# The rotation of the queries: three of its five vector steps computed on GpSimd, the factor 2^-13 moved into the tables

## The chip, the cores and the metric

The kernel runs on one core of a Trainium2 chip. The metric is the device time of one execution in microseconds (us). A core has TensorE (PE in the profile) for matrix products, VectorE (DVE), ScalarE (ACT) and GpSimd (POOL) for work along rows, and a queue of transfers issued by SyncE (SP). The engines run side by side, each through its own list of instructions in order; an instruction whose input is not ready holds up everything behind it on its engine.

## The reference

The reference is a trunk of two layers over 2048 tokens of width 1024. Each layer normalises its input, multiplies it by one wide matrix `w_in`, and splits the result into a recurrent branch, an attention branch and a pooling branch. These are gated, joined, multiplied by `w_out` and added to the input. A last normalisation follows the second layer.

The change concerns the attention branch, cut here to what matters:

```python
q = (rms_norm(c_q, q_norm_g) @ w_uq).reshape(B, S, MLA_HEADS, QK_NOPE_DIM + QK_ROPE_DIM)
q_nope = q[..., :QK_NOPE_DIM]
q_rope = apply_rope(q[..., QK_NOPE_DIM:], cos, sin)
...
s = (einsum(q_nope, k_nope) + einsum(q_rope, k_rope)) * scale   # causal, softmax, times v
```

There are six heads with 64 plain and 32 rotated elements each. The rotation takes the two halves x1, x2 of the 32 and returns x1 cos - x2 sin and x1 sin + x2 cos, with tables of cos and sin over the positions.

## The kernel before, in words

Numbers of 32 bits are split into two halves of 16 bits, a high and a low part, and a product is the sum of three products of 16-bit halves. So nearly every result that PE leaves in PSUM is followed by two operations: ACT writes the high part, DVE subtracts it from the value and writes the low part.

Tokens are worked in four chunks of 512 (C), heads in three pairs (p). A layer runs in stages: the products with `w_in` (`zgroup`, line 397), with the branches' own work interleaved; then the keys, values and queries of the attention; then scores, softmax and values for each chunk of queries and pair of heads (`scores`, `finish`), with the output product interleaved. Before the scores of a chunk and pair, `row_max` (lines 799 to 821) computes a bound for each row's maximum: PE multiplies high parts, DVE takes maxima straight from PSUM (L804, L806), and the result goes through DRAM into row 96 of the tile `kq`.

`q_rope(x, tag)` (line 763 on) makes the rotated part of the queries for one pair of heads and two chunks. It is called six times per layer: once in `early`, which runs between the last products with `w_in`; once in the list `rest` behind them; and four times in `later_queries`, during the first attention units. Its steps:

1. SP loads the tables `ct` and `sn`, each 128x512 in 32 bits.
2. PE makes eighteen products into the PSUM tile `qrp` (L772).
3. DVE swaps the halves of each group of 32 rows, from PSUM into the SBUF tile `qsw` (L780).
4. DVE multiplies `qrp` by 2^-13 and by `ct` (L781, the first product), and `qsw` by 2^-13 and by `sn` (L782, the second product), and adds the two into `ct` (L783, the sum).
5. ACT writes the sum's high part into the tile `pr` (L785), DVE the low part (L786).
6. SP sends `pr` to its rows of `kq` in four transfers (L788), each with both parts.

The rotation of the keys, `krope`, runs once per layer and already multiplies on GpSimd (L631, L632). GpSimd's other work is small: gains times weights (L221), ones beside the values (L748), and the fill of row 96 in `head_tiles` (L711).

The order on each engine is not simply that of the program text. `spawn`, `tick` and `between` interleave generators while the program is written down, and the framework's planner then places the instructions of each engine by priority and by when its cost model thinks that their inputs are ready. Thus the trace shows other instructions between the steps of one rope. The tiles `ct`, `sn`, `qsw`, `pr` and many others share seven buffers (tag `t`).

Of the kernel before, what the change touches and what calls it, by code (L numbers as in the profile page):

```python
# [14 lines left out]
ALU = mybir.AluOpType  # L15
# [31 lines left out]
RUNITS = [((p, c), (p, c + 1)) for p in range(3) for c in range(0, NC, 2)]  # L47
# [8 lines left out]
def body(nc, tc, a, ctx):  # L56
# [11 lines left out]
    def T(name, dt=F32):  # L68
        return tp.tile([128, 512], dt, tag="t", bufs=7, name=name)

    def PS(tag, name):
        return psum.tile([128, 512], F32, tag=tag, bufs=BANKS[tag], name=name)
# [317 lines left out]
    def zgroup(st, m, c, few):  # L390
        w, sc = st["zw"][m]
        zbank[0] += 1
        ps = PS("mm" if few else ("mm", "mm", "po", "mm", "su")[zbank[0] % 5], "zps")
        n = 0
        for k in range(KD):
            for i, j in PASSES:
                nc.tensor.matmul(  # L397
                    ps[:], w[:, i, k, :], st["h"](j, k, c), start=n == 0, stop=n == 3 * KD - 1
                )
                n += 1  # L400
            if k % FINE == FINE - 1:
                between()
        return ps, sc

    def layer(st):
# [357 lines left out]
        def q_rope(x, tag):  # L763
            units = RUNITS[x]
            ps = PS(tag, "qrp")
            ct, sn, qs = T("ct"), T("sn"), T("qsw")
            nc.sync.dma_start(ct[:], a["rq"][x, 0])
            nc.sync.dma_start(sn[:], a["rq"][x, 1])
            for n in range(9):
                k, (i, j) = n // 3, PASSES[n % 3]  # L770
                for u, (p, c) in enumerate(units):
                    nc.tensor.matmul(  # L772
                        ps[64 * u : 64 * u + 64, :],
                        wq[p][:, i, k, 128:192],
                        hats["q"][:, j, k, CS[c]],
                        start=n == 0,
                        stop=n == 8,
                        tile_position=(0, 64 * u),
                    )
            nc.vector.stream_shuffle(qs[:], ps[:], mask=swap)  # L780
            nc.vector.scalar_tensor_tensor(ct[:], ps[:], 2.0 ** -13, ct[:], ALU.mult, ALU.mult)  # L781
            nc.vector.scalar_tensor_tensor(sn[:], qs[:], 2.0 ** -13, sn[:], ALU.mult, ALU.mult)  # L782
            nc.vector.tensor_tensor(ct[:], ct[:], sn[:], ALU.add)  # L783
            t = tp.tile([128, 2, 512], F16, tag="t", bufs=7, name="pr")
            nc.scalar.activation(t[:, 0, :], ct[:], AF.Copy)  # L785
            nc.vector.tensor_tensor(t[:, 1, :], ct[:], t[:, 0, :], ALU.subtract)  # L786
            for g, (p, c, h) in enumerate([(p, c, h) for p, c in units for h in range(2)]):
                nc.sync.dma_start(kq[p][64:96, h, 2:4, CS[c]], t[32 * g : 32 * g + 32, :, :])  # L788

# [52 lines left out]
        def early():  # L842

            for t in range(6):
                values_of(t, "ax")
                yield 1
                yield 1
            head_tiles(0, big, "A")
            for c in range(NC):
                keys(0, c, "ax")  # L850
                yield 1
            for c in range(2):
                while lat.get(("q", c)) != "done":
                    yield 1
                query(0, c, "ax")
                yield 1
            q_rope(0, "ax")
            yield 1
            for qc in range(2):
                yield from row_max(qc, 0, 3)  # L860
                maxed.add((qc, 0))
# [46 lines left out]
        for g, (m, c) in enumerate(groups):  # L908
# [13 lines left out]
            ps, sc = zgroup(st, m, c, g < g1)  # L922
# [31 lines left out]
        for p in (1, 2):  # L954
            for n in range(5):
                rest += [lambda p=p, n=n: keys(p, n, bank())] if n < NC else []
                rest += [lambda t=5 * p + n + 1: values_of(t, bank())]
            if p < QE:
                rest += [lambda p=p: query(p, 0, bank()), lambda p=p: query(p, 1, bank())]
                rest += [lambda p=p: q_rope(2 * p, bank()), lambda p=p: have.add((p, 0))]  # L960
# [308 lines left out]
def arrange(x, norm_g, w_in, conv_w, conv_b, w_rg, b_rg, w_ig, b_ig, lru_lambda,  # L1269
            q_norm_g, w_uq, kv_norm_g, w_ukv, w_pool, pool_scale, w_out, final_norm_g):  # L1270
    f = np.float32
    A = lambda v: np.ascontiguousarray(np.asarray(v))
    ins, par = {}, {}
    ins["x"] = A(np.asarray(x)[0])
    w_in = np.asarray(w_in)

    starts = [0, 128, 256, 384, 512, 640, 1152, 1280, 768, 896, 1024, 1824, 1952, 2080, 2208, 1440, 1568, 1696]
    wk_ = w_in.reshape(L, KD, 128, w_in.shape[2]).transpose(0, 2, 1, 3)
    ins["win"] = A(np.stack([wk_[:, :, :, s : s + 128] for s in starts], axis=1))
    ins["wkr"] = A(wk_[:, :, :, 1408:1440])  # L1280
    par["ng"] = A(np.asarray(norm_g).reshape(L, KD, 128).transpose(2, 0, 1))
    prm = np.zeros((128, L, 3, 8), f)
    per = lambda v: np.asarray(v).reshape(L, 3, 128).transpose(2, 0, 1)
    for t in range(4):
        prm[:, :, :, t] = per(np.asarray(conv_w)[:, t])
    for i, v in enumerate((conv_b, b_rg, b_ig, lru_lambda)):
        prm[:, :, :, 4 + i] = per(v)

    gb = prm[:, :, :, 5:7].reshape(2, 64, L, 3, 2)
    prm[:, :, :, 5:7] = gb.transpose(4, 1, 2, 3, 0).reshape(128, L, 3, 2)  # L1290
    par["prm"] = prm
    wg = np.zeros((L, 3, 128, 2, 128), f)
    for g, w in enumerate((np.asarray(w_rg), np.asarray(w_ig))):
        for h in range(6):
            c = slice(64 * g, 64 * g + 64)
            wg[:, h // 2, 0:64, h % 2, c] = wg[:, h // 2, 64:128, h % 2, c] = w[:, h]
    ins["wg"] = wg
    wp = np.zeros((L, 2, 128, 128), f)
    for g in range(4):
        r = 64 * (g % 2)  # L1300
        wp[:, g // 2, r : r + 64, r : r + 64] = np.asarray(w_pool)[:, g]
    ins["wp"] = wp
    par["pscl"] = A(np.asarray(pool_scale).reshape(L, 2, 128).transpose(2, 0, 1))
    par["kg"] = A(np.asarray(kv_norm_g).reshape(L, 2, 128).transpose(2, 0, 1))
    par["qg"] = A(np.asarray(q_norm_g).reshape(L, 3, 128).transpose(2, 0, 1))
    ins["fgb"] = A(np.broadcast_to(np.asarray(final_norm_g), (128, D)))
    uq = np.asarray(w_uq).reshape(L, 3, 128, 3, 2, 96).transpose(0, 3, 2, 1, 4, 5)
    ins["wuq"] = A(
        np.concatenate(
            [uq[..., :64].reshape(L, 3, 128, 3, 128), uq[..., 64:].reshape(L, 3, 128, 3, 64)], axis=-1  # L1310
        )
    )
    ukv = np.asarray(w_ukv).reshape(L, 2, 128, 6, 128).transpose(0, 2, 1, 3, 4)
    ins["wukv"] = A(
        np.concatenate(
            [ukv[..., :64].reshape(L, 128, 2, 384), ukv[..., 64:].reshape(L, 128, 2, 384)], axis=-1
        )
    )
    ins["wout"] = A(np.asarray(w_out).reshape(L, KD, 128, D))

    pos = np.arange(S, dtype=f)
    inv = f(10000.0) ** (-np.arange(0, 32, 2, dtype=f) / f(32))
    ang = (pos[:, None] * inv[None, :]).astype(f)
    cos, sin = np.cos(ang).astype(f).T, np.sin(ang).astype(f).T
    c32, s32 = np.concatenate([cos, cos]), np.concatenate([-sin, sin])
    two = lambda t, c: np.tile(t[:, C * c : C * c + C], (2, 1))
    ins["rq"] = A(np.stack([np.stack([np.concatenate([two(t, c) for _, c in u]) for t in (c32, s32)]) for u in RUNITS]))
    rows = lambda t: A(t.reshape(32, NC, C).transpose(1, 0, 2).reshape(128, C))
    ins["cosk"], ins["sink"] = rows(c32), rows(s32)
    p = np.arange(128)  # L1330
    tri = np.where(p[None, :] > p[:, None], f(-1e36), f(0)).astype(f)
    ins["masks"] = A(np.concatenate([np.eye(128, dtype=f), tri, tri.T], axis=1))
    rc = np.zeros((128, 2, 17), f)
    for g, w in enumerate((2, 4, 8, 16)):
        r = 64 * (g % 2)
        rc[r : r + 64, g // 2, 0:16] = w / np.minimum(np.arange(1, 17), w)
        rc[r : r + 64, g // 2, 16] = 1.0 / w
    par["rcnt"] = rc
    ins["par"] = A(np.concatenate([par[n].reshape(128, -1) for n in PAR], axis=1))
    return ins  # L1340
# [22 lines left out]
```

## Time and profile before

| What | Value |
|---|---|
| median of 3 runs | 1963.67 us (1960.27 to 1965.01) |
| profiled execution, own time | 1963.13 us |
| its span, first to last instruction | 1961.3 us |
| mean granted TensorE clock | 0.991 |
| PE busy | 1890.0 us, 96% |
| DVE busy | 1439.5 us, 73% |
| ACT busy | 1163.4 us, 59% |
| POOL busy | 45.6 us, 2%, 38 instructions |

A busy time is the sum of the stretches in which the engine computed. Matrix products overlap in the engine's pipeline, so PE's busy time says when PE had work, not that it was at its peak. A wait is written `A <- B`: the instruction A was released by B. The tile before the arrow `<-` inside a name is the one written, those behind it are read.

### The profile page before, as it was taken

How to read it: one execution, taken by the hardware profiler on the slowest of the kernel's cores; microseconds unless marked ns; L12 is line 12 of the kernel's file. 1: busy time of each engine (PE TensorE's matmuls, PEld its weight loads, DVE VectorE, ACT ScalarE, POOL GpSimd, SP SyncE). 2: the span in 40 equal slices, each digit the busy share in tenths (PEclk: the TensorE clock that was granted, in tenths of full speed). 3: DMA queues.
4: the chain of work that ended last, by engine and by line, in shares of the span. 5: the costliest groups of instructions: out<-in, count | busy, mean ns of one | idle time of the engine just before them, and what ended most of it. 6: DMA issues, size and time to landing. Idle time of an engine off the chain costs nothing. (4 is left out here: it accounts for less than half of the span.)

```text
span 1961.3 us, 32926 instructions
## 1 busy us (share of the span) xinstructions
PE 1890.0 (96%) x12352; PEld 981.0 (50%) x12352; DVE 1439.5 (73%) x3310; ACT 1163.4 (59%) x2095; POOL 45.6 (2%) x38
## 2 busy tenths in 40 slices
PE   8999999999889999999999999999998999999998
PEld 4444444444455555555454444444444555555553
DVE  6757788767898787774385567878687977987745
ACT  8877877644355455465386678775434644644641
POOL 0000000010000000000000000001010000000000
PEclk8999999999999999999999999999999999999999
DMA  6313242212453121122741223331234621421444
GB/s 204 119 49 113 78 139 100 62 33 63 102 167 128 44 92 43 46 76 68 250 152 63 81 93 99 116 106 46 49 76 103 200 77 44 151 87 55 162 152 145
DMA packets 125281, 197.75 MB, mean 101 GB/s; under 512 B 18752, under 2 KB 41536, under 8 KB 125120
## 3 DMA queue, kind: packets, MB, share of 16 engines
q1 hardware_dynamic: 125120, 195.64, 31.8%
q8 instruction: 97, 1.59, 0.3%
q14 instruction: 64, 0.52, 0.1%
HBM read 124.59 MB, written 55.26 MB: 92 GB/s over the span
## 5 line engine op out<-in xcount | busy, mean ns | idle before, releaser
L397 PEld LDWEIGHTS <-zw 128*128 128x128 f16 x3456 | 336.3, 99 | 395.8 <-issue 21.3
L1030 ACT ACTIVATE p<-sps,tiny,sig 128x512 f32<-128x512 f32 x480 | 321.5, 709 | 327.2 <-PE sps L1027 174.9
L397 PE MATMUL zps<-hA,zw 128*128 128x512 f16 x1728 | 396.3, 383 | 0.3 <-DVE hA L355 0.2
L397 PE MATMUL zps<-hB,zw 128*128 128x512 f16 x1728 | 382.6, 379 | 0.0
L1104 PE MATMUL ops<-wo,yb 128*128 128x512 f16 x1536 | 368.5, 379 | 6.4 <-DVE xr L1096 4.8
L1031 DVE TENSOR_TENSOR pl<-p 128x1024 f16<-128x1024 f32 x240 | 254.0, 1059 | 126.3 <-ACT p L1030 100.3
L1104 PEld LDWEIGHTS <-yb 128*128 128x128 f16 x1536 | 144.5, 97 | 171.2 <-issue 8.2
L804 DVE TENSOR_REDUCE mx<-pm 128x1 f32<-128x512 f32 x288 | 192.6, 683 | 21.9 <-PE pm L799 21.8
L1025 PE MATMUL sps<-kq 97*128 97x512 f16 x480 | 167.0, 348 | 3.0 <-ACT p L1030 2.8
L1026 PE MATMUL sps<-kq 96*128 96x512 f16 x480 | 166.6, 347 | 0.0
L1027 PE MATMUL sps<-kq 96*128 96x512 f16 x480 | 165.7, 345 | 0.0
L799 PE MATMUL pm<-kq 96*128 96x512 f16 (+3 forms) x496 | 151.0, 345 | 5.0 <-DVE mx L804 2.5
L1044 PE MATMUL av<-zw,p 128*128 128x129 f16 (+1 forms) x1632 | 140.2, 214 | 5.2 <-ACT ar L994 5.2
L1044 PEld LDWEIGHTS <-p 128*128 128x128 bf16 x1632 | 108.5, 98 | 30.3 <-PE sps L1029 1.0
L806 DVE CUSTOM_DVE_ANT_0 pm<-pm,mkq 128x128 f32<-128x128 f32 (+1 forms) x208 | 101.1, 495 | 12.7 <-PE pm L799 11.8
L1044 PE MATMUL av<-zw,pl 128*128 128x65 f16 x1632 | 92.9, 194 | 1.7 <-DVE pl L1031 1.7
L1044 PEld LDWEIGHTS <-pl 128*128 128x128 f16 x1632 | 75.1, 98 | 12.2 <-DVE pl L1031 8.3
L1026 PEld LDWEIGHTS <-kq 96*128 96x128 f16 x480 | 47.2, 98 | 43.4 <-issue 5.1
L1027 PEld LDWEIGHTS <-kq 96*128 96x128 f16 x480 | 47.1, 98 | 43.6 <-issue 1.9
L1025 PEld LDWEIGHTS <-kq 97*128 97x128 f16 x480 | 46.6, 97 | 44.0 <-issue 4.2
L485 ACT ACTIVATE lsa<-pg,gp 64x512 f32<-64x512 f32 x96 | 65.2, 679 | 1.6
L1049 PE MATMUL av<-zw,p 128*128 128x64 f16 x336 | 64.8, 193 | 0.0
(300 smaller groups left out, 2613.2 us busy)
## 6 DMA issues: line engine op xcount, KB each, us to landing
xk<-x SPq DMA_DIRECT2D x80, 256.0 KB
raw<-win SPq DMA_DIRECT2D x72, 256.0 KB
raw<-wout SPq DMA_DIRECT2D x64, 256.0 KB
yr<-y SPq DMA_DIRECT2D x64, 256.0 KB
xr<-x SPq DMA_DIRECT2D x56, 256.0 KB
x<-xr SPq DMA_DIRECT2D x56, 256.0 KB
sg<-sg SPq DMA_DIRECT2D x48, 256.0 KB
kq<-pq SPq DMA_DIRECT2D x96, 128.0 KB
```

Source lines behind the costliest of these rows:

```text
L397: nc.tensor.matmul(ps[:], w[:, i, k, :], st["h"](j, k, c), start=n == 0, stop=n == 3 * KD - 1)
L485: nc.scalar.activation(t_[o], pg[h, :], AF.Tanh, scale=0.5, bias=gp[h, l, j, b : b + 1])
L799: nc.tensor.matmul(pm[:, 0:n], t[0:96, h, 2, q0 : q0 + 128], t[0:96, h, 0, s * C : s * C + n], start=True, stop=True)
L804: nc.vector.tensor_reduce(m, pm[:], AX.X, ALU.max)
L806: nc.vector.tensor_tensor_reduce(out=pm[:, 0:n], in0=pm[:, 0:n], in1=mkq[:, C - n : C], op0=ALU.add, op1=ALU.max, scale=1.0, scalar=-3.0e3 ...
L1025: nc.tensor.matmul(ps[:, o:C], t[0:97, h, 0, ks], t[0:97, h, 2, qs], start=True, stop=False)
L1026: nc.tensor.matmul(ps[:, o:C], t[0:96, h, 0, ks], t[0:96, h, 3, qs], start=False, stop=False)
L1027: nc.tensor.matmul(ps[:, o:C], t[0:96, h, 1, ks], t[0:96, h, 2, qs], start=False, stop=not diag)
L1030: nc.scalar.activation(pw_[:, h, o:C], ps[:, o:C], AF.Exp, scale=sig[:, 4:5], bias=tiny[:, 1:2])
L1031: nc.vector.tensor_tensor(pl[:, :, o:C], pw_[:, :, o:C], ph[:, :, o:C], ALU.subtract)
L1044: nc.tensor.matmul(acc[h][:, c - 64 * lo : c + 65], w, v[:, 64 - 64 * lo : QB], start=first and n == 0 and j == 0, stop=end and n == 1 and ...
L1104: nc.tensor.matmul(ps[:], yb[:, j, k, 128 * (n // 2) : 128 * (n // 2) + 128], wo[n % 2, k][:, i, :], start=m == 0, stop=m == 3 * KD - 1,)
```

## The change

In `q_rope` the second product, the sum and the low part go from DVE to GpSimd. The swap and the first product, which read PSUM, stay on DVE; the high part stays on ACT. The factor 2^-13 is multiplied into the tables on the host when the inputs are laid out, so that both products become plain multiplications of two tensors. 2^-13 is a power of two, so the tables lose no digits.

```diff
             nc.vector.stream_shuffle(qs[:], ps[:], mask=swap)
-            nc.vector.scalar_tensor_tensor(ct[:], ps[:], 2.0 ** -13, ct[:], ALU.mult, ALU.mult)
-            nc.vector.scalar_tensor_tensor(sn[:], qs[:], 2.0 ** -13, sn[:], ALU.mult, ALU.mult)
-            nc.vector.tensor_tensor(ct[:], ct[:], sn[:], ALU.add)
+            nc.vector.tensor_tensor(ct[:], ps[:], ct[:], ALU.mult)
+            nc.gpsimd.tensor_tensor(sn[:], qs[:], sn[:], ALU.mult)
+            nc.gpsimd.tensor_tensor(ct[:], ct[:], sn[:], ALU.add)
             t = tp.tile([128, 2, 512], F16, tag="t", bufs=7, name="pr")
             nc.scalar.activation(t[:, 0, :], ct[:], AF.Copy)
-            nc.vector.tensor_tensor(t[:, 1, :], ct[:], t[:, 0, :], ALU.subtract)
+            nc.gpsimd.tensor_tensor(t[:, 1, :], ct[:], t[:, 0, :], ALU.subtract)
...
-    ins["rq"] = A(np.stack([np.stack([np.concatenate([two(t, c) for _, c in u]) for t in (c32, s32)]) for u in RUNITS]))
+    ins["rq"] = A(np.stack([np.stack([np.concatenate([two(t, c) for _, c in u]) for t in (c32 * f(2.0 ** -13), s32 * f(2.0 ** -13))]) for u in RUNITS]))
```

## Rows read from the trace of the kernel before

**Rows 1.** Busy time of the engines: us, share of the span, instructions.
```profile
PE 1890.0 (96%) x12352; PEld 981.0 (50%) x12352; DVE 1439.5 (73%) x3310; ACT 1163.4 (59%) x2095; POOL 45.6 (2%) x38
```
**Rows 2.** Stretches: length, busy us per engine, clock, DMA share, GB/s.
```profile
core 0: us, PE busy (x) PEld busy (x) DVE busy (x) ACT busy (x) POOL busy (x), PEclk, DMA share, GB/s
465.00:590.00 125.00, 113.79 (x818) 59.67 (x816) 110.25 (x293) 58.76 (x107) 7.33 (x3) 0.99 0.48 126
1431.00:1556.00 125.00, 113.84 (x820) 59.84 (x818) 110.29 (x294) 58.64 (x107) 7.34 (x3) 0.99 0.47 126
...
480.00:510.00 30.00, 26.64 (x134) 12.06 (x132) 29.76 (x95) 9.16 (x18) 3.51 (x1) 0.94 0.39 94
```
**Rows 3.** PE's waits from 465 to 590 us: total us, times, longest.
```profile
PE av L1044 <- ACT ar L994: 2.6, 3, 1.4
PE vps L741 <- DVE ct L781: 1.5, 1, 1.5
...
PE qrp L772 <- DVE pq L722: 1.3, 1, 1.3
PE pm L799 <- DVE mx L804: 1.1, 2, 0.7
PE qps L758 <- DVE ct L781: 1.0, 1, 1.0
...
PE pn L245 <- ACT sqh L238: 0.6, 1, 0.6
```
**Rows 4.** Lines of `q_rope` on DVE: count, ns (min/median/max), first and last start, form.
```profile
L781 DVE SCALAR_TENSOR_TENSOR ct<-qrp,ct x12: 670/687/695, 471.0 to 1538.1; 128x512 f32<-128x512 f32 x12
...
L782 DVE SCALAR_TENSOR_TENSOR sn<-qsw,sn x12: 681/683/693, 471.6 to 1539.3; 128x512 f32<-128x512 f32 x12
...
L783 DVE TENSOR_TENSOR ct<-ct,sn x12: 649/684/692, 472.8 to 1540.6; 128x512 f32<-128x512 f32 x12
...
L786 DVE TENSOR_TENSOR pr<-ct,pr x12: 682/691/693, 474.6 to 1542.7; 128x512 f16<-128x512 f32 x12
```
**Rows 5.** POOL's groups by form: busy us, mean ns, idle before and releaser.
```profile
L221 POOL TENSOR_TENSOR raw<-raw,par 128x384 f32<-128x384 f32 x14 | 14.0, 1003 | 1130.0 <-DVE zsc L375 984.7 <-DMA raw<-wukv 135.4 <-DMA raw<-wuq 4.7
L632 POOL TENSOR_TENSOR ksw<-ksw,sn 128x512 f32<-128x512 f32 x2 | 3.4, 1710 | 0.0
L631 POOL TENSOR_TENSOR kr<-kr,ct 128x512 f32<-128x512 f32 x2 | 3.2, 1618 | 3.2 <-DVE ksw L630 3.2
```
**Rows 6.** Instructions around `krope` in order of time: start us, length us.
```profile
394.89 2.35 DVE L602 TENSOR_TENSOR ckh<-raw,ckh 128x512 f16<-128x512 f32 x2
...
395.06 1.62 POOL L631 TENSOR_TENSOR kr<-kr,ct 128x512 f32<-128x512 f32 x1 [1.88 <-DVE ksw L630]
...
396.65 1.71 POOL L632 TENSOR_TENSOR ksw<-ksw,sn 128x512 f32<-128x512 f32 x1
```
**Rows 7.** Instructions behind rope 1, all engines.
```profile
472.04 3.51 POOL L711 MEMSET kq<- 1x4096 f16 x1 [34.54 <-PE zps L397]
...
475.28 2.63 SPq L788 DMA_DIRECT2D kq<-pr  x4
...
478.59 0.33 PE L799 MATMUL pm<-kq 96*128 96x128 f16 x2
```
**Rows 8.** Instructions at ropes 4 and 6, in order of time.
```profile
540.29 0.76 DVE L780 STREAM_SHUFFLE qsw<-qrp 128x512 f32<-128x512 f32 x1
...
544.05 0.63 ACT L785 ACTIVATE pr<-ct 128x512 f16<-128x512 f32 x1 [6.79 <-DVE ct L783]
...
545.15 0.19 PE L1044 MATMUL av<-zw,p 128*128 128x65 f16 x1 [1.35 <-ACT ar L994]
...
571.64 0.69 DVE L781 SCALAR_TENSOR_TENSOR ct<-qrp,ct 128x512 f32<-128x512 f32 x1 [0.31 <-DMA ct<-rq]
...
574.85 0.63 ACT L785 ACTIVATE pr<-ct 128x512 f16<-128x512 f32 x1 [1.91 <-DVE ct L783]
```

## The prediction

> **What bounds the kernel now.** I read the busy times first. PE is busy 96% of the span, DVE 73%, POOL 2% [rows 1]: an edit to DVE work can pay only where PE waits for DVE. The stretches come next. The twelve calls of `q_rope` lie in two stretches of 125 us, one per layer. In each PE is idle 11.2 us (125 less 113.8) while DVE is busy 110 [rows 2]. So all that the change can take from waiting is 22.4 us, 1.1% of the time, and PE's other work stays. DVE is full only in 480 to 510 (29.8 of 30), where the row maxima run; there PE's clock averaged 0.94, that is 3.6 us at its lower level (1.2 GHz), a loss of 1.8 us [rows 2]. Last I read whom PE waits for in the first stretch [rows 3]: 2.6 us for ACT's copies of the finished accumulators (`ar`), 2.5 for the rope's own first product (`ct`, which stays on DVE), 1.3 for the low part `pq`, 1.1 for row maxima, 0.6 for `sqh`. The second layer's stretch repeats the first almost instruction for instruction, so I work out one layer and double it.
>
> **The change, part by part.** I number the ropes of a layer 1 to 6; their shuffles start at 470, 502, 525, 540, 556 and 571 us.
>
> Removed from DVE: second product, sum and low part, 0.683 + 0.684 + 0.691 = 2.06 us per rope [rows 4], 24.7 us in all, 12.3 per layer. The first product becomes a plain multiply of the same 128x512 out of PSUM; the row for a product with the factor is 0.687, for a two-tensor operation 0.684 [rows 4], so I count it as nothing. Scaling the tables is done outside the kernel; shapes and the two table DMAs stay, also nothing.
>
> Added to POOL: 36 operations of 128x512. The nearest rows are two such products in `krope`, 1.62 and 1.71 us, and a 128x384 product at 1.00 [rows 5]. But the long ones ran beside DVE. Two low parts `L602`, two-tensor operations of the size in rows 4, would take 2 x 0.68; they took 2.35 [rows 6]: DVE stood about 1 us, and the POOL operations were waiting in turn. The 3.3 us from 395.06 to 398.36 hold two POOL products, one `L602`, and the rest of another; that leaves about 1.1 for a POOL product alone. Ends: 1.1 and 1.7 each. I take 1.1 plus what it waits for DVE. The f16 output of the low part is shown by no row on POOL; the same two ends apply, and I take 1.1. POOL then works 40 to 61 us more and has room for that.
>
> The price is contention. What rows 6 show is a DVE operation with two SBUF inputs standing still while POOL computes. In a rope's neighbourhood such operations are `L602`, `L587`, `L1031`, `L998`; the row maxima, `L722` and `L750` read PSUM. The Trainium skill says the same more sharply (SBUF — State Buffer, section Who interferes with whom): a DVE instruction with two SBUF inputs and a GpSimd one that reads SBUF exclude each other for a whole instruction, while a DVE instruction with one SBUF input is left alone. By that rule, if each of the 36 met such an instruction at its start, DVE would lose 36 x 1.1 = 40 us for 24.7 saved. The trace has only the two shown as a clean case.
>
> Now the ropes, one at a time.
>
> Rope 1 loses. Behind it on DVE stand only two-input operations, `L602` twice and `L587`, then `L239`. Before, DVE ran these three and the rope's three from 471.6 to 475.2 (first starts of `L782` and `L786` [rows 4] and the latter's length), six in 3.6 us, 0.6 apart. After, three of 0.6 alternate with POOL's 1.1 of second product and sum, and `L239` meets the low part: about 4.3. `L587`, which ACT's `sqh` and through it PE wait for [rows 3], is 0.6 to 1 late: +0.7.
>
> Rope 2 falls into the full stretch, but its second product, sum and low part ran after the last PE wait there (the 1.5 for `ct` [rows 3]), and DVE catches up soon after: 0.
>
> Rope 3 starts with DVE waiting for the table's DMA, as before; then `pl` (`L1031`) and POOL's sum ask together. If POOL goes first, `pq` comes 0.6 early, if `pl` goes first, 0.6 late: 0.
>
> Rope 4 gains. Here DVE put other work ahead of the second product, ACT stood 6.79 us at the high part, and the `ar` copies queued behind it held PE for 1.35 [rows 8]. POOL has no such queue: shuffle end at 541.05 [rows 8], second product to 542.15, sum to 543.25, high part at 543.3 instead of 544.05: -0.7.
>
> Rope 5 has a `pl` just after the shuffle; POOL waits for it, and the sum ends about where it did: 0.
>
> Rope 6 is like rope 4: the first product ends at 572.33, the sum would end at 573.5, and the high part start 1.3 earlier than its 574.85 [rows 8], and the PE wait for `ar` behind it loses about half a microsecond: -0.5.
>
> A layer gives +0.7 - 0.7 - 0.5 = -0.5, the kernel -1.0 us. By bounds: if every POOL operation takes 1.7, ropes 4 and 6 gain nothing and rope 1 costs 1.5, so +3 in all; with all locks falling well, ropes 1 to 3 give 2 more per layer, so -5. The profiled execution took 1963.13 us for its span of 1961.3; -1.0 makes 1962.1. The median of the runs shown, 1963.67, is 0.5 above that execution, so I forecast 1962.7.
>
> The DMAs that carry the rope to `kq` wait for both halves. On SP's queue four of them per rope stand ahead of the key DMAs. The high part's ACT instruction likewise has `ar` copies, `sqh` and `pq` behind it. I count those waits in the ropes above.
>
> **The rivals.**
>
> *Relief reaches PE (faster).* The operations around the rope are put in order per engine by a planner, and the DVE rows show foreign instructions between a rope's steps. If the new order puts PSUM readers beside POOL's three, rope 1 frees its 2 us, the row maxima of 480 to 510 come 2 us earlier, and the shorter wait for `ct` spares the low clock: 2 + 1.8 per layer, with ropes 4 and 6 another 1.2, so 2 x 5 = -10 us: 1953.7. For it: DVE is full there. Against: the 3.4 us that PE is idle in that stretch [rows 2] are all the waiting there is to take, and the standing of rows 6.
>
> *POOL's own queue (slower).* At rope 1 the 3.51 us fill of `head_tiles` (`L711`) begins at 472.04, 1 us after the shuffle [rows 7]; in the second layer as well. POOL's three operations share that queue. If the fill gets between them, for instance while the low part waits for ACT's high part, the rope's DMAs, issued from 475.28, go out up to 3.5 us late. The first row maximum, at 478.59, has at most about a microsecond to spare [rows 7], so the full DVE stretch starts 2.5 us late and `sqh` may wait behind the high part too: +2.5 + 1 + 0.7 - 0.5 = 3.7 per layer, about +7: 1970.7. It decides once the fill stands ahead of the sum or the low part in POOL's order. Against: the ropes come earlier in the program, and the fill has no hurry: only the scores, after the row maxima, read it.
>
> *The lock wins (slower).* If the two-input DVE operations mostly lose, ropes 1 and 2 cost DVE 6 x 1.1 = 6.6 for 4.1 saved in its full stretch, +2.5 per layer, and the `pl` of ropes 3, 5 and 6, which PE's `av` wait for, 0.4 each: 2 x 3.7 = +7.4: 1971.1. That is the place where the skill's rule would decide. Against: most DVE operations of these stretches, the row maxima above all, read PSUM.
>
> **How the numbers follow.** A measurement of this kernel tells 0.3%, 5.9 us, from no change: under 1957.8 is faster, over 1969.6 slower. Forecast of no change: 0.45 (its own range 1957 to 1968). Relief: 0.31. Fill in POOL's queue: 0.15. Lock: 0.09. So faster 0.31, same 0.45, slower 0.24. The range reaches to 1952 and 1971: all but the ends of the three rivals.
>
> **What would show it.** Right: POOL 86 to 107 us busy, DVE about 1415 plus what it stands; POOL's products at 1.1 beside PSUM readers and longer beside two-input operations; `L602` and `L587` stretched over 1 us at rope 1; ACT's wait at the high part of rope 4 ending 0.7 earlier, its `ar` copies too. Wrong: PE's idle time in the two stretches changed by more than 3 us each; the fill between a rope's steps; a POOL operation well over 1.7 us, or the low part with f16 far from the products; or a change outside the two stretches, which nothing here foresees.

## The result: 1996.9 us, slower by 32 us

The changed kernel takes 1996.86 us (median of 4 runs, 1992.81 to 1998.68) against 1964.34 for the kernel before (1960.27 to 1965.08): ratio 1.0162, 95% interval 1.0150 to 1.0173, or +32 us. I had forecast 1962.7 and a range to 1971. The profiled execution took 1995.8 us for a span of 1994.0, at a mean clock of 0.984. Below, differences are worked out from the ratios on 1964 us; each has an interval of some 2 to 4 us either way, and the difference of two experiments one of 4 to 5.

Busy times of the changed kernel, to hold against [rows 1]:

```profile
PE 1900.3 (95%) x12352; PEld 985.2 (49%) x12352; DVE 1433.1 (72%) x3274; ACT 1164.8 (58%) x2095; POOL 93.4 (5%) x74
```

DVE lost 36 instructions worth 24.7 us [rows 4], yet is busy only 6.4 us less: 18 us came back as instructions that took longer. PE is busy 10 us more for the same number of matmuls.

The stretches with the ropes, and six microseconds inside the first (columns as in [rows 2]):

```profile
465.00:590.00 125.00, 105.76 (x657) 52.29 (x656) 92.16 (x240) 47.74 (x86) 29.55 (x20) 0.92 0.40 106
...
1449.00:1574.00 125.00, 106.35 (x658) 53.15 (x657) 93.42 (x244) 48.68 (x88) 29.77 (x21) 0.93 0.40 106
...
579.00:585.00 6.00, 2.87 (x15) 1.52 (x15) 3.35 (x10) 1.39 (x3) 0.00 (x0) 0.50 0.97 290
```

Where [rows 2] show 0.99, the granted clock averages 0.92 and 0.93, and PE gets through 657 matmuls in 125 us instead of 818. The loss arises here: against before, the gating products (`L1008`) run 20.1 us late from the end of layer 0's ropes to the end of that layer, the shuffle of layer 1's first rope comes 18.1 late, and the gating products behind its last rope 33.6; the span is 32.7 longer. Both layers repeat one pattern.

PE's waits in layer 0, 465 to 640 us (columns as in [rows 3]):

```profile
PE pm L799 <- DVE y L1008: 4.9, 1, 4.9
PE sps L1025 <- ACT p L1030: 3.9, 1, 3.9
PE kps L730 <- ACT raw L580: 2.7, 1, 2.7
...
PE pm L799 <- DMA kq<-pr: 2.0, 1, 2.0
```

None of these four is in [rows 3] at such a size. Two of them can be followed instruction by instruction.

Rope 1 (start, length, engine, idle time before and its releaser):

```profile
471.97 1.27 POOL L782 TENSOR_TENSOR sn<-qsw,sn 128x512 f32<-128x512 f32 x1 [33.80 <-DVE qsw L780]
472.23 3.23 DVE L602 TENSOR_TENSOR cqh<-raw,cqh 128x512 f16<-128x512 f32 x2
...
473.32 1.59 POOL L783 TENSOR_TENSOR ct<-ct,sn 128x512 f32<-128x512 f32 x1
474.94 0.63 ACT L785 ACTIVATE pr<-ct 128x512 f16<-128x512 f32 x1 [3.79 <-DMA kq<-kr]
474.97 3.51 POOL L711 MEMSET kq<- 1x4096 f16 x1
475.48 0.67 ACT L580 ACTIVATE raw<-zps,zsc 128x512 f32<-128x512 f32 x1
...
476.20 2.46 PE L730 MATMUL kps<-ckh,wk 128*128 128x512 f16 x6 [2.73 <-ACT raw L580]
...
478.56 1.38 POOL L786 TENSOR_TENSOR pr<-ct,pr 128x512 f16<-128x512 f32 x1
...
479.96 1.36 SPq L788 DMA_DIRECT2D kq<-pr  x2
```

POOL's sum and DVE's two `L602` held each other up: 1.59 us instead of 1.27, and 3.23 instead of 1.37. ACT stood 3.79 us at the high part until the sum was there (the releaser named is a DMA long issued; the sum ended at 474.91). Behind it on ACT stood `L580`, which frees the PSUM bank that PE wants: 2.73 us of PE. DVE's `L587`, which reads what ACT writes behind these two, began 5.8 us after the shuffle's start, against 3.6 in the kernel before; 1.38 of that it waited for ACT. The fill `L711` then went ahead of the low part, and the transfers left at 479.96 instead of 475.28 [rows 7].

Rope 5, 90 us later:

```profile
562.42 0.58 SPq L767 DMA_DIRECT2D ct<-rq  x1
...
563.10 0.38 SPq L768 DMA_DIRECT2D sn<-rq  x1
...
567.39 1.86 POOL L783 TENSOR_TENSOR ct<-ct,sn 128x512 f32<-128x512 f32 x1
...
569.28 0.63 ACT L785 ACTIVATE pr<-ct 128x512 f16<-128x512 f32 x1 [3.63 <-POOL ct L783]
...
569.99 1.16 POOL L786 TENSOR_TENSOR pr<-ct,pr 128x512 f16<-128x512 f32 x1 [0.74 <-ACT pr L785]
...
571.17 4.11 SPq L788 DMA_DIRECT2D kq<-pr  x4
...
575.38 1.31 SPq L724 DMA_DIRECT2D kq<-pq  x2
...
576.73 0.59 SPq L989 DMA_DIRECT2D sg<-sg  x1
...
581.32 0.75 DVE L1008 SCALAR_TENSOR_TENSOR y<-pt,gbf,sg 128x512 f32<-128x512 f32 x1 [5.15 <-DMA wo<-wo]
...
582.13 0.37 PE L799 MATMUL pm<-kq 96*128 96x256 f16 x1 [4.87 <-DVE y L1008]
```

SP issues the tables, and its next instruction is the rope's first transfer, which waits for the low part until 571.15. SP issues nothing for 7.7 us. Behind stands the load of `sg`, which the gating product needs (the releaser named, `wo`, is a neighbour on the same queue that this product does not read). DVE stands 5.15 us, PE 4.87, and the clock is at its lower level, 1.2 GHz, from 578.9 to 585.7. Before, `sg` left ahead of this rope's transfers. SP stood for them then too, 6.0 us:

```profile
554.33 0.36 SPq L989 DMA_DIRECT2D sg<-sg  x1
560.71 2.62 SPq L788 DMA_DIRECT2D kq<-pr  x4
```

The planner had turned the two round.

SP's waits, 515 to 600 us, after and then before (us, times, longest):

```profile
SPq L788 <- POOL pr L786: 29.9, 4, 8.3
```

```profile
SPq L788 <- DVE pr L786: 5.9, 1, 5.9
SPq L788 <- DVE pq L722: 5.9, 1, 5.9
...
SPq L788 <- DVE ar L998: 2.5, 2, 1.4
```

So SP stood 30 us for four ropes' transfers, and 14 before. From shuffle to first transfer, ropes 1 to 6 took 4.9, 8.5, 8.1, 5.1, 5.0 and 6.4 us before, and take 9.0, 6.6, 7.9, 7.2, 8.5 and 8.0 after: four are later, two are not.

### The profile page after: what moved, and what is told of

The parts are those of the page before. It is cut to its first block, busy times and chain, and to the rows that moved or that the text cites. A ratio compares the mean times of both kernels' runs of the same rounds, so it can differ in the third digit from the quotient of the medians.

```text
span 1994.0 us, 33006 instructions
## 1 busy us (share of the span) xinstructions
PE 1900.3 (95%) x12352; PEld 985.2 (49%) x12352; DVE 1433.1 (72%) x3274; ACT 1164.8 (58%) x2095; POOL 93.4 (5%) x74
## 3 DMA queue, kind: packets, MB, share of 16 engines
q8 instruction: 97, 1.59, 0.3%
## 5 line engine op out<-in xcount | busy, mean ns | idle before, releaser
L221 POOL TENSOR_TENSOR raw<-raw,par 128x384 f32<-128x384 f32 (+1 forms) x20 | 16.1, 818 | 1057.3 <-DMA raw<-wukv 975.1
```

## The experiments

Two theories. *Queue*: the chain through POOL makes the rope late, and SP's queue, which stands for its transfers, makes other transfers late. *Lock*: POOL's reads of SBUF stop DVE, and that alone costs the time. The result shows signs of both. Some expectations call the first the theory of the late rope and the second contention.

### Parts of the change

**e1_tables** keeps the new tables and leaves all steps on DVE. Against the changed kernel:

```diff
-            nc.gpsimd.tensor_tensor(sn[:], qs[:], sn[:], ALU.mult)
-            nc.gpsimd.tensor_tensor(ct[:], ct[:], sn[:], ALU.add)
+            nc.vector.tensor_tensor(sn[:], qs[:], sn[:], ALU.mult)
+            nc.vector.tensor_tensor(ct[:], ct[:], sn[:], ALU.add)
...
-            nc.gpsimd.tensor_tensor(t[:, 1, :], ct[:], t[:, 0, :], ALU.subtract)
+            nc.vector.tensor_tensor(t[:, 1, :], ct[:], t[:, 0, :], ALU.subtract)
```

> Changed tables and plain products, everything still on DVE. The two theories (the queue theory: GpSimd's longer chain makes the rope late and the planner's other order puts its transfers and copies ahead of others; the lock theory: GpSimd's reads of SBUF stop DVE) both say 1964 +- 4 us, since nothing is on GpSimd and each engine's order is that of before. The form theory (a plain product of two tensors with one operand in PSUM, or the scaled tables, is what costs): a good part of the 32 us, 1975 us or more.

1963.21 against 1963.60, ratio 1.0002 (0.9991 to 1.0013). Tables and plain products cost nothing that 2 us would show; what follows is due to GpSimd.

**e3_low** and **e4_product** move one operation each to GpSimd, the low part or the second product. Against e1_tables, e3_low first:

```diff
-            nc.vector.tensor_tensor(t[:, 1, :], ct[:], t[:, 0, :], ALU.subtract)
+            nc.gpsimd.tensor_tensor(t[:, 1, :], ct[:], t[:, 0, :], ALU.subtract)
```

```diff
-            nc.vector.tensor_tensor(sn[:], qs[:], sn[:], ALU.mult)
+            nc.gpsimd.tensor_tensor(sn[:], qs[:], sn[:], ALU.mult)
```

> Only the low part on GpSimd, with the new tables. Lock theory: a third of the operations, a third of the loss, 1972 to 1976 us. Queue theory: the rope's four transfers still wait for GpSimd's low part, and that for the fill of row 96 that may stand ahead of it: 1967 to 1979 us, with SP's waits for the tile pr released by POOL as in after.

> Only the second product on GpSimd, with the new tables. Lock theory: a third of the loss, 1972 to 1976 us. Queue theory: the product runs beside DVE's first product, the sum waits some 0.6 us for it and nothing behind the sum is later than that; 1964 +- 6 us, unless the planner's order comes out otherwise.

1970.23 (ratio 1.0033, 1.0021 to 1.0044) and 1969.25 (1.0029, 1.0013 to 1.0044), so +6.5 and +5.7 us. **e9_nolow** is the changed kernel with the low part back on DVE:

```diff
-            nc.gpsimd.tensor_tensor(t[:, 1, :], ct[:], t[:, 0, :], ALU.subtract)
+            nc.vector.tensor_tensor(t[:, 1, :], ct[:], t[:, 0, :], ALU.subtract)
```

> Second product and sum on GpSimd, low part on DVE, new tables. Contention theory: two operations of three, +12 to +22 us over before. Theory of the late rope: SP no longer waits for GpSimd behind a fill, and the later sum costs only at ropes whose transfers meet others: +3 to +12 us.

1982.22, ratio 1.0091 (1.0076 to 1.0106), +17.9. Neither theory fits alone: the single operations land in the queue theory's ranges and below the lock's, the pair in the lock's and above the queue's. And in e9 the wait for `sg` is there again (4.4 us) though SP no longer stands for POOL itself.

### The reads alone

**e2_beside** is the kernel before with three POOL operations beside each rope.

```diff
-            nc.vector.scalar_tensor_tensor(ct[:], ps[:], 2.0 ** -13, ct[:], ALU.mult, ALU.mult)
+            nc.vector.scalar_tensor_tensor(ct[:], ps[:], 2.0 ** -13, ct[:], ALU.mult, ALU.mult); d4, i4 = dz[:].rearrange("p (a b) -> p a b", a=4), idt[:].unsqueeze(1).broadcast_to([128, 4, 128]); nc.gpsimd.tensor_tensor(dz[:], qs[:], qs[:], ALU.mult); nc.gpsimd.tensor_tensor(d4, i4, i4, ALU.add); nc.gpsimd.tensor_tensor(d4, i4, i4, ALU.mult)
```

> The kernel before with three extra GpSimd operations of two tensors, 128x512, beside each rope, whose results nobody reads; the order of the other engines is that of before. Lock theory: GpSimd's operations alone slow DVE, 1979 to 1997 us. Queue theory: no instruction of the rope waits for them, 1964 +- 6 us, although some of DVE's operations beside them come out longer (after showed about 8 us per layer).

1983.76, ratio 1.0093 (1.0075 to 1.0110): +18.3 us, where the queue theory said 6 at most. Rope 1 and its neighbours in this kernel:

```profile
471.67 1.04 POOL L781 TENSOR_TENSOR dz<-qsw 128x512 bf16<-128x512 f32 x1 [33.72 <-DVE qsw L780]
472.01 1.25 DVE L782 SCALAR_TENSOR_TENSOR sn<-qsw,sn 128x512 f32<-128x512 f32 x1
...
472.79 2.81 POOL L781 TENSOR_TENSOR dz<-idt 128x512 bf16<-128x512 f32 x2
...
473.18 1.52 DVE L602 TENSOR_TENSOR cqh<-raw,cqh 128x512 f16<-128x512 f32 x1
...
474.63 1.52 DVE L783 TENSOR_TENSOR ct<-ct,sn 128x512 f32<-128x512 f32 x1
...
475.66 3.51 POOL L711 MEMSET kq<- 1x4096 f16 x1
476.07 0.68 DVE L602 TENSOR_TENSOR cqh<-raw,cqh 128x512 f16<-128x512 f32 x1
```

Three DVE operations of 0.68 take 1.25, 1.52 and 1.52 while POOL computes, and the next one, beside the fill, 0.68 again. The kernel's DVE is 12 us busier:

```profile
PE 1900.3 (96%) x12352; PEld 985.5 (50%) x12352; DVE 1451.5 (73%) x3310; ACT 1163.9 (59%) x2095; POOL 88.0 (4%) x74
```

The order on SP, DVE, ACT and PE is that of before, instruction by instruction, so these 18 us come from the three operations: 12 us of standing on DVE, and a lower clock in the rope stretches (0.97 and 0.96 instead of 0.99).

### The three causes apart

Three kernels leave the second product, sum and low part out, so that DVE has the relief of the change, and add one thing each to the text. Their results are not the rotation. The planner orders SP, DVE, ACT and PE in e11 as in e10; e10 against before, and e12 against e10, have a new order.

```diff
-            nc.gpsimd.tensor_tensor(sn[:], qs[:], sn[:], ALU.mult)
-            nc.gpsimd.tensor_tensor(ct[:], ct[:], sn[:], ALU.add)
...
-            nc.gpsimd.tensor_tensor(t[:, 1, :], ct[:], t[:, 0, :], ALU.subtract)
+            nc.gpsimd.memset(t[:, 1, :], 0.0)
```

**e10_less** is this alone.

> The changed kernel with the second product and the sum left out and the low part replaced by a fill with zeros on GpSimd, which nothing has to wait for: DVE's relief alone, its result is not the rotation. If relief reaches PE: 1950 to 1957 us. If DVE was not what held PE: 1963 +- 3 us. Both theories of the loss (GpSimd's reads beside DVE; the later rope) expect no loss here.

1954.14, ratio 0.9944 (0.9928 to 0.9959): -11.0 us. But this is more than DVE's relief: with the steps gone, the rope itself is shorter (2.0 to 5.0 us from shuffle to first transfer, where before had 4.9 to 8.5), and the order is new. So e10 shows that leaving the steps out is worth 11 us, not which of the three brings them.

**e11_less_beside** adds three POOL operations whose results nobody reads, as in e2. Against e10_less:

```diff
+            nc.gpsimd.tensor_tensor(dz[:], qs[:], sn[:], ALU.mult); d4, i4 = dz[:].rearrange("p (a b) -> p a b", a=4), idt[:].unsqueeze(1).broadcast_to([128, 4, 128])
+            nc.gpsimd.tensor_tensor(d4, i4, i4, ALU.add)
...
-            nc.gpsimd.memset(t[:, 1, :], 0.0)
+            nc.gpsimd.memset(t[:, 1, :], 0.0); nc.gpsimd.tensor_tensor(d4, i4, i4, ALU.mult)
```

> As the kernel with the second product, sum and low part left out, plus three GpSimd operations of two tensors, 128x512, per rope, whose results nobody reads; the other engines' order is the same as there. Contention theory: the reads cost here what they cost beside the kernel before, +15 to +20 us over that kernel. Theory of the late rope: not more than +6 us, since DVE has 2 us less to do per rope.

1963.45, ratio 0.9993 (0.9983 to 1.0003): +9.6 us over e10, again with the others' order unchanged. DVE's busy time rises from 1420.1 to 1431.8, the 12 us of e2 once more. Here they cost half as much; DVE has 19 us less to do, which may be the reason, but no run shows it.

**e12_less_chain** replaces the three by fills, which read nothing, in the same places of the chain:

```diff
+            nc.gpsimd.memset(qs[:], 0.0); nc.gpsimd.memset(qs[:], 0.0); nc.gpsimd.memset(qs[:], 0.0)
+            nc.gpsimd.memset(ct[:], 0.0); nc.gpsimd.memset(ct[:], 0.0); nc.gpsimd.memset(ct[:], 0.0)
...
+            nc.gpsimd.memset(t[:, 1, :], 0.0); nc.gpsimd.memset(t[:, 1, :], 0.0); nc.gpsimd.memset(t[:, 1, :], 0.0)
```

> As the kernel with the three steps left out, but in their place GpSimd fills of some 1.3 us together, which write and read nothing, with the same waits in the chain: swap, fills, fills of the first product's tile, high part, transfers. Theory of the late rope: +10 to +20 us over the kernel with the steps left out. Contention theory: +-3 us.

1974.98, ratio 1.0050 (1.0031 to 1.0068): +20.8 us over e10, while DVE's busy time is 1423.4, 3 us more. Here is a longer chain without the lock, and the wait of rope 5 in after returns, at rope 6:

```profile
575.01 1.13 POOL L783 MEMSET ct<- 128x512 f32 x2
...
576.17 0.63 ACT L785 ACTIVATE pr<-ct 128x512 f16<-128x512 f32 x1 [1.93 <-POOL ct L783]
...
576.83 2.62 SPq L788 DMA_DIRECT2D kq<-pr  x4
...
579.54 1.38 SPq L826 DMA_DIRECT2D kq<-nm  x2
...
580.97 0.44 SPq L989 DMA_DIRECT2D sg<-sg  x1
...
585.15 0.75 DVE L1008 SCALAR_TENSOR_TENSOR y<-pt,gbf,sg 128x512 f32<-128x512 f32 x1 [6.36 <-DMA sg<-sg]
...
585.96 0.48 PE L799 MATMUL pm<-kq 96*128 96x384 f16 x1 [6.05 <-DVE y L1008]
```

DVE stands 6.36 us for `sg`, ordered behind the rope's transfers and a row bound (`L826`), and PE 6.05. The same rope in the kernel before:

```profile
575.62 0.43 SPq L989 DMA_DIRECT2D sg<-sg  x1
...
576.96 2.60 SPq L788 DMA_DIRECT2D kq<-pr  x4
```

The transfers leave at the same time in both; only `sg` has changed sides. In all, e12's ropes take 8.5, 5.3, 5.2, 4.9, 5.1 and 4.9 us from shuffle to first transfer: against e10 each of them is later, against before only the first by more than 0.1 us. So at rope 6 it is the planner's new order that costs, not a rope later than in before. The 20.8 us hold both, the longer chain and the new order, and this pair does not part them.

### SP out of the rope

The remaining runs issue transfers from POOL instead of SP.

```diff
-                nc.sync.dma_start(kq[p][64:96, h, 2:4, CS[c]], t[32 * g : 32 * g + 32, :, :])
+                nc.gpsimd.dma_start(kq[p][64:96, h, 2:4, CS[c]], t[32 * g : 32 * g + 32, :, :])
```

**e5_poolq** does this in the changed kernel, **e8_before_poolq** in the kernel before.

> The changed kernel, with the rope's four transfers issued by GpSimd behind its own low part instead of by SP. Queue theory (the rope's late transfers hold up SP's other transfers, sg above all): SP no longer stands for POOL, the wait of the gating product for sg (5.2 us in after) and the fall of the clock behind it go: 1975 to 1988 us. If the late rope costs by itself, through what reads it, or by the planner's order: 1993 to 2000 us, as after.

> Control: the kernel before with the rope's four transfers issued by GpSimd instead of SP. Queue theory: SP stands little for the rope here, 1964 +- 4 us. If a transfer issued by GpSimd is itself a gain or a loss it shows here.

1978.82, ratio 1.0078 (1.0061 to 1.0096), 17 us under after; and 1952.50, ratio 0.9948 (0.9933 to 0.9964), 10 us under before. The expected gain came, but the expectation for the control was wrong: the rope's transfers on SP cost something in the kernel before as well. So 10 of e5's 16.5 us can be had without the change, and only 6 are its own. With POOL issuing, the change still costs 25.5 us (e5 against e8). In both pairs the planner's order of all engines is new. Among the runs with the whole rotation e8 is the fastest, and it beats both kernels.

**e13_after_sgpool** and **e13_before_sgpool** move only the load of `sg`, in the changed kernel and in the one before.

```diff
-            nc.sync.dma_start(sg[:], sgd[l][p, :, CS[qc]])
+            nc.gpsimd.dma_start(sg[:], sgd[l][p, :, CS[qc]])
```

> The changed kernel, with only the loads of sg issued by GpSimd instead of SP; DVE's order is nearly that of after. Queue theory: the wait of the second unit's gating product for sg goes in layer 0 and with it a fall of the clock, 5 to 8 us of the 32: 1988 to 1992 us. Otherwise 1996 +- 3 us.

> Control: the kernel before with the loads of sg issued by GpSimd instead of SP. There the gating products did not wait for sg: 1964 +- 3 us.

1986.52, ratio 1.0119 (1.0102 to 1.0135), 8 us under after, with the wait of that gating product down from 5.15 to 1.77 us; and 1972.21, ratio 1.0037 (1.0024 to 1.0049), 7 us over before. The same edit helps where `sg` stood behind a late rope and hurts where it did not. Why it hurts there I did not follow up.

That left open how much of e12's 20.8 us is SP's queue. **e10_less_pq**, **e11_less_beside_pq** and **e12_less_chain_pq** are e10, e11 and e12 with the rope's transfers issued by POOL.

> Base of the second group: second product, sum and low part left out (the low part a fill with zeros), and the rope's four transfers issued by GpSimd. Both theories: some 11 us under the kernel with SP's transfers and the same steps left out, or no change if that gain and the relief are the same time: 1941 to 1955 us.

> The same base with the three GpSimd operations of two tensors beside, results unused. Contention theory: +8 to +12 us over the base, as with SP's transfers (+9.6), since the port does not know who issues transfers; the transfers also stand behind these operations in GpSimd's own queue here.

> The same base with the GpSimd fills in the chain. With SP's transfers the chain cost 20.8 us. Queue theory: most of it was SP standing for the rope, so 2 to 9 us over the base here. If the late rope costs through what reads it or through what it holds up elsewhere (ACT's high part, buffers): 15 to 21 us again.

1952.24 (ratio 0.9943, 0.9921 to 0.9964), 1970.16 (1.0025, 1.0011 to 1.0039) and 1955.81 (0.9953, 0.9936 to 0.9969). The chain costs 2 us by the ratios, 3.6 by the medians, not 20.8; the interval of this difference is 5 us either way. The orders differ here too. In e12_less_chain_pq `sg` leaves ahead of the rope:

```profile
565.08 0.32 SPq L989 DMA_DIRECT2D sg<-sg  x1
...
565.30 1.09 POOL L783 MEMSET ct<- 128x512 f32 x2
...
567.97 2.11 POOL L788 DMA_DIRECT2D kq<-pr  x4 [1.57 <-ACT pr L785]
```

and the first stretch (465 to 640) has its clock and PE's work back; e12_less_chain, then e12_less_chain_pq:

```profile
465.00:640.00 175.00, 157.58 (x1147) 84.21 (x1146) 139.43 (x352) 82.82 (x151) 33.13 (x55) 0.96 0.44 121
```

```profile
465.00:640.00 175.00, 166.55 (x1249) 89.28 (x1247) 148.75 (x376) 86.68 (x159) 45.91 (x79) 0.99 0.43 123
```

The reads cost 16 us here by the ratios; DVE's busy time rises by 13.9 (1418.8 to 1432.7), about as in e11. The 16 is loose: PE and DVE have a slightly different order, and the ten runs of e11_less_beside_pq go from 1961.87 to 1972.92, and the profiled pair (spans 1960.1 and 1949.1) says 11.

The ledger, in us against before:

| | SP issues the rope's transfers | POOL issues them |
|---|---|---|
| rotation on DVE | 0 | -10.2 |
| three steps left out | -11.0 | -11.2 |
| + reads beside | +9.6 | +16.1 |
| + chain without reads | +20.8 | +2.0 |
| remainder, both at once | +12.4 | +8.4 |
| the change | +31.8 | +15.3 |

The second row is what the change would cost if DVE were relieved and nothing put in place; the third and fourth are what the beside and the chain kernels add to that; the fifth is what is then missing to the change. With POOL issuing, leaving the three steps out gains only 1 us on e8. So e10's 11 us and e8's 10 us are not two gains; I take them for the same one, a rope that is sooner off SP, which the equal ends suggest but no run shows by itself. The remainder stays open. With e2's price of the reads (18.3) instead of e11's it would be 4 in the first column. Another candidate, not shown either: reads lengthen the chain (POOL's sum took up to 1.86 us, the low part up to 2.10), and a longer chain costs more at a queue.

## Why the prediction was wrong

**The step that failed** is "The DMAs that carry the rope to `kq` wait for both halves ... I count those waits in the ropes above." I saw SP's queue and priced what stood behind it at nothing, rope by rope, in the order of before. The order did not stay: the planner moved `sg` behind the rope's transfers, and four of layer 0's six ropes became later. Against e10, the runs put 20.8 us on chain and order with SP issuing and 2.0 to 3.6 with POOL issuing; in the changed kernel itself, 16.5 us go when POOL issues, 6 more than in the kernel before. The term was not nothing; its size differs by kernel, and how much of it is the order and how much the standing stays open. Rope 5, which I set at 0, holds the clearest piece (4.87 us of PE); rope 4, at -0.7, took 2.1 us longer to its transfers.

**POOL's price.** Lines of the three operations in after (count, ns min/median/max):

```profile
L782 POOL TENSOR_TENSOR sn<-qsw,sn x12: 1265/1268/1426, 472.0 to 1570.4; 128x512 f32<-128x512 f32 x12
...
L783 POOL TENSOR_TENSOR ct<-ct,sn x12: 1262/1267/1862, 473.3 to 1571.8; 128x512 f32<-128x512 f32 x12
...
L786 POOL TENSOR_TENSOR pr<-ct,pr x12: 1152/1156/2102, 478.6 to 1573.8; 128x512 f16<-128x512 f32 x12
```

I took 1.1 and named 1.7 as the other end; alone they take 1.27, 1.27 and 1.16, and POOL's 93.4 us lies in the 86 to 107 I gave. That was a small miss. But 0.5 to 0.6 us more than DVE needs, three times in one chain, was added to no queue.

**The lock** is the second term that was too small, and the one that the runs show most cleanly, since e2 and e11 change no other engine's order. It exists as [rows 6] showed: 12 us of DVE standing for 36 operations, a third of a microsecond each, not the 1.1 that 36 full meetings would give. It costs 9.6 to 18.3 us. In my sum it stood as +0.7 per layer at rope 1 and 0 elsewhere; as a rival I gave it 7.4 with a chance of 0.09. Both were low: I priced the standing at ropes 1, 2, 3, 5 and 6, and left out the lower clock that came with it in e2 (0.97 and 0.96). By the Trainium skill (SBUF — State Buffer, section Who interferes with whom) only GpSimd instructions that read SBUF meet such DVE instructions, not those that only write it. The fills agree: 108 more of them in e12 than in e10 left DVE's busy time within 3.3 us.

**Relief reaches PE** has the right size in e10, -11.0 against my -10, but that is not shown to be my mechanism. I had the low clock spared; e10 still has 3.4 us of it in layer 0's rope stretch and 6.8 in layer 1's, where before had 3.4 in each. And with POOL issuing, leaving the steps out gains 1 us. So the match is at least partly luck. In any case the change brought the reads and the chain along.

**POOL's own queue** came in part. The fill did go between the sum and the low part of rope 1. But the first row maximum, at 484.30, did not wait for it; the 2.73 us of PE at that rope came from ACT's queue, where `L580` stood behind a high part that waited for POOL's sum. I had named that queue ("`ar` copies, `sqh` and `pq` behind it") and counted only `sqh` there, in the +0.7 of rope 1.

**The bound.** I set the gain's limit by the 22.4 us that PE was idle, and took the loss from the rivals one at a time. A loss has no such limit: PE's idle time in 465 to 640 rose from 12.1 to 25.6 us, and on top the clock fell.

## What to carry to other kernels

When a step goes to a slower engine, follow its last result into the issuing queue, and list what stands behind it there in the new order, not in the old one; a planner that sees the step on another engine can write another order for all of them. If the rope's transfers must wait, let them wait on a queue where nothing urgent follows. Before moving elementwise work to GpSimd, price three things apart: relief, reads beside DVE's two-input operations, and the longer chain; here they were about -11, +10 to +18, and +2 to +21 by who issued the transfers, and they did not add up to the whole.

## What the runs showed that I had not expected

Issuing 48 transfers from GpSimd instead of SP gained 10 us in a kernel whose text was otherwise unchanged (e8). POOL spends 0.54 us on each:

```profile
L788 POOL DMA_DIRECT2D kq<-pr x48 | 25.5, 538 | 132.3 <-DVE pr L786 90.4 <-DVE m L814 23.5 <-DVE r L996 18.4
```

The Trainium skill (DMA: Bandwidth & Descriptors, section Issuing engines are not separate DMA queues) says that issuing from several engines saves only the time on the sequencer. Here SP is spared the issues, 0.61 us each, but also the waits that stood ahead of its other issues, and the order is new; the runs don't divide the gain among these three.

PE's stalls came with a second price. In after the granted clock goes to its lower level, 1.2 GHz, in five places from 465 to 640 us, 24 us in all, against one place of 3.4 us before. Four of the five begin during a wait of PE of 2.0 to 4.9 us or up to 1.2 us behind it; ahead of the fifth, at 517, PE had only waits under 1 us. That the waits cause the falls is read from this neighbourhood alone.

A fill on GpSimd takes 0.52 us for 128x512, of 16 or 32 bits alike, and 3.51 for one row of 4096.
